# A hybrid decoder layer on one core: bounded expert gathers, an fp32 half of the input projection, and one-hot matrices written by GpSimd

## The chip, the cores and the metric

The kernel runs on one core of a Trainium2 chip. The metric is the device time of one execution in microseconds (us), median of several runs. The engines are TensorE (PE; its weight loads are listed as PEld), VectorE (DVE), ScalarE (ACT), GpSimd (POOL) and SyncE (SP), which here issues most of the DMAs.

## The reference, cut to what matters

256 tokens of width 2048 go through a token mixer and then through an expert mixer. Matrices are fp32.

```python
h = modulate(rms_norm(x, g_pre_mix), sh1, sc1)          # shifts, scales, gates: silu(c) @ w_mod + b_mod
proj = h @ w_in                                          # 2048 x 4096
lru_x, lru_g, conf_v, conf_g = split(proj)               # 1024 columns each
y_lru = rg_lru(conv4(lru_x)) * gelu(lru_g)               # scan over time
z = silu(layer_norm(conv31(conf_v * sigmoid(conf_g))))
x = x + gt1 * rms_norm(concat([y_lru, z]) @ w_out)
h = modulate(rms_norm(x, g_pre_ffn), sh2, sc2)
q = (h @ wq)                                             # 8 heads, 2 halves of 128
# per head: top 16 of each half's 128 keys, then top 16 of the 256 sums
expert = row * 128 + col                                 # 8 heads x 16 slots = 128 experts a token
act = einsum(h, u_table[expert]); w = softmax(gates) * gelu(act)
x = x + gt2 * rms_norm(sum(w * v_table[expert]))         # u, v tables: 16384 x 2048 each
```

## The kernel before

**Numbers.** TensorE runs plain fp32 matmuls at a low rate, so large products split each fp32 matrix: a rounded high part (`split`: ScalarE copies, line 94) and the rest as a low part (VectorE subtracts, line 95). A product is three matmuls per 128 rows of the contraction: high by high, high by low, low by high (lines 351, 352, 354 and 765, 766, 768).

**Modulation and projection (to about 355 us).** `modchunk` and `modfull` stream `w_mod` through fp32 matmuls (lines 251, 276). `hchunk` writes `xn`, the modulated input, and its halves `hH` and `hL`. Ten of the 32 column tiles of `w_in` are begun early (`begin`); the other 22 go through `proj`, which takes two slabs of eight contraction tiles each. `slab` loads 512 KB into a buffer of `fring` (four buffers, and a fifth lent from `yT`), splits it into buffers of `Hring` and `Lring`, and issues 24 matmuls. Between slabs, `modstep` advances the modulation. `conf` turns two tiles into a gated tile and runs 31 taps of a convolution on VectorE (line 422); `lru` does the recurrence; `confln` the layer norm. The outputs `zc` lie in the upper half of the same memory as `xn`, the running sum `zs` in its first tile. Then comes `w_out`.

**First half of the experts (about 484 to 1234 us).** Instead of gathering whole rows, the kernel multiplies all 16384 experts densely on the first 1536 columns of `u` (`upiece`: 128 expert rows in two pieces of six contraction tiles, into the table `S` of 128 x 128 scores a token), and gathers only the last 512 columns: per slot one indirect DMA from GpSimd (`gathers`, line 704, 128 rows of 2 KB) and one multiply-and-sum on VectorE (`dot`, line 710). A planner, executed while the program is written out, sets the order by hand for VectorE: every piece calls `fill` (304 calls), which counts calls in `clock[0]`, grants the gathers a credit in `clock[2]`, and then places steps of the top-k search (`topk`) and dots into the rest of the piece's time; a dot comes at least `LAG` = 3 calls after its gather. GpSimd runs its queue in order and starts a gather as soon as its index column `ei` is written and the last dot on its buffer is done. Buffers: six in `guS` and 30 lent from rows of `S` not yet written; `free` is a queue, first in first out; `retire` takes lent buffers back.

**Weight stage (about 1234 to 1415 us).** For four tokens at a time, `extract` loads the slots' column indices (`cold`) on all partitions, forms the column-by-slot one-hot matrix `cb`, on GpSimd for even chunks (line 917) and on ScalarE in two passes for odd ones (lines 914, 915), multiplies it by `S` (line 920, fp32) and lets VectorE pick the slot's row (line 924). `wbuild`, one group of 16 tokens later, needs the transpose, slots by columns: TensorE transposes `cb` (line 937), ScalarE copies it out (line 939), VectorE writes the weighted row one-hot `At` (line 944), TensorE multiplies (line 945, fp32), and ScalarE puts the token's weights into `S` (line 946). `mods` is the rest of the last modulation vector, 20 steps of a 512 KB load and four matmuls; from the ninth chunk on one step goes with every chunk.

**Second half (about 1415 us to the end).** `S`, now the weights, multiplies the dense part of `v` (line 1023); 512 columns are gathered (line 996) and added on VectorE (line 1005).

Outside the stretches that are ordered by hand, a scheduler orders each engine's instructions by priority when the program is built.

## Time and profile before

| | |
|---|---|
| median of 3 runs | 2002.36 us (2001.26 to 2014.05) |
| profiled execution, its own time | 1990.23 us |
| its span | 1988.5 us |
| TensorE busy, share of the span | 1827.9 us, 92% |
| VectorE | 1530.5 us, 77% |
| ScalarE | 972.3 us, 49% |
| GpSimd | 674.8 us, 34% |

The span runs from the first to the last instruction. Busy times are sums over stages with different limits, so the shares say little alone. Durations of matmuls include their pipeline; the distance from start to start is what one costs in a row. An fp32 matmul is listed as two records.

### The profile page before, as it was taken

Reading aid. Unit: us, or ns where it says so; the run is one execution under the profiler, and the core shown is the slowest. Engines: PE = TensorE matmul, PEld = TensorE weight load, DVE = VectorE, ACT = ScalarE, POOL = GpSimd, SP = SyncE. Lnnn points to the kernel's source line nnn. Section 1 sums busy time; section 2 is a strip of 40 time slices with the busy share of each in tenths; the row PEclk is TensorE's granted clock in tenths of the full one; section 3 lists DMA queues with packets and bytes.
Section 4 is the critical chain, followed back from the end, with each engine's and each line's share of the span. In section 5 each row is a group of like instructions: output and inputs, shape, how many; then the busy total and the mean of one; then the engine's idle time right before and its main releaser. Section 6 shows DMA issues by size and latency. Waiting matters only on the chain.

```text
span 1988.5 us, 34804 instructions
## 1 busy us (share of the span) xinstructions
PE 1827.9 (92%) x12408; PEld 1580.1 (79%) x12408; DVE 1530.5 (77%) x3834; ACT 972.3 (49%) x1512; POOL 674.8 (34%) x577
## 2 busy tenths in 40 slices
PE   7897999898949699999899999999999999999996
PEld 3675787685949699999899999789877777778874
DVE  3249999755729489999787775789788888888887
ACT  3244434743625355555455555567544444544453
POOL 0000000000061432323543442224377666666662
PEclk8999999998979799999999999999999999999998
DMA  9988868686776677778898887742499898888884
GB/s 326 373 313 320 281 229 317 262 287 245 230 239 195 216 252 256 261 244 280 289 300 274 290 289 221 212 139 81 131 319 329 327 324 310 313 300 316 311 303 161
DMA packets 174799, 530.07 MB, mean 267 GB/s; under 512 B 20753, under 2 KB 44449, under 8 KB 167201
## 3 DMA queue, kind: packets, MB, share of 16 engines
q1 hardware_dynamic: 132656, 391.50, 57.8%
q0 software_dynamic: 40960, 134.25, 20.0%
q8 instruction: 97, 1.59, 0.3%
q10 hardware_dynamic: 1008, 2.10, 0.3%
q14 instruction: 78, 0.63, 0.1%
HBM read 521.40 MB, written 6.37 MB: 265 GB/s over the span
## 4 chain that ended last, share of the span: by engine, by line
PE 55%; issue 16%; POOL 11%; DMA 9%; DVE 5%; ACT 2%; another core or an unknown queue 1%; POOLq 0%; SPq 0%; ACTq 0%; DVEq 0%
PE acc L765 11%; PE acc L766 11%; PE acc L768 11%; POOL S L996 7%; PE acc L354 4%; PE acc L351 4%; PE acc L352 3%; PE W L945 3%; PE modps L276 3%; PE G L920 2%; DMA PF<-in_w_mod_dram 2%; POOL sl L996 2%; DMA PF<-in_w_in_dram 2%; POOL sh L996 2%; DVE PF L422 2%
## 5 line engine op out<-in xcount | busy, mean ns | idle before, releaser
L765 PE MATMUL acc<-sh,sb 128*128 128x256 f32 x1792 | 453.4, 288 | 36.8 <-issue 23.2
L766 PE MATMUL acc<-sl,sb 128*128 128x256 f32 x1792 | 452.1, 287 | 0.3 <-issue 0.3
L765 PEld LDWEIGHTS acc<-sh,sb 128*128 128x128 f32 x1792 | 349.3, 195 | 42.0 <-issue 25.1
L766 PEld LDWEIGHTS acc<-sl,sb 128*128 128x128 f32 x1792 | 349.3, 195 | 2.3 <-issue 2.2
L94 ACT ACTIVATE sb<-R 128x768 fp32r<-128x768 f32 (+2 forms) x203 | 196.8, 970 | 262.3 <-PE acc L766 115.2
L95 DVE TENSOR_TENSOR sb<-S,sb 128x768 fp32r<-128x768 f32 (+3 forms) x272 | 219.8, 809 | 130.7 <-ACT sb L94 106.1
L768 PE MATMUL acc<-sh,sb 128*128 128x256 f32 x1792 | 269.3, 285 | 9.9 <-issue 9.3
L94 ACT ACTIVATE sb<-S 128x768 fp32r<-128x768 f32 (+3 forms) x274 | 207.4, 759 | 140.0 <-PE acc L766 85.9
L996 POOL DMA_INDIRECT S<-in_vg_dram,ei x158 | 212.7, 1346 | 112.3 <-DVE R L1005 82.5
L768 PEld LDWEIGHTS acc<-sh,sb 128*128 128x128 f32 x1792 | 240.0, 194 | 10.1 <-issue 9.1
L704 POOL DMA_INDIRECT R<-in_ug_dram,ei x111 | 112.5, 1013 | 390.7 <-DMA R<-in_ud_dram 252.3
L95 DVE TENSOR_TENSOR sb<-R,sb 128x768 fp32r<-128x768 f32 (+1 forms) x160 | 150.2, 939 | 109.7 <-ACT sb L94 64.7
L704 POOL DMA_INDIRECT S<-in_ug_dram,ei x145 | 147.0, 1014 | 246.8 <-DVE R L710 156.3
L1023 PE MATMUL o<-sl,sb 128*128 128x512 f32 x900 | 221.4, 394 | 9.9 <-DVE sl L95 8.2
L1023 PE MATMUL o<-sh,sb 128*128 128x512 f32 x888 | 219.0, 395 | 10.1 <-DVE sh L95 9.3
L1023 PEld LDWEIGHTS o<-sl,sb 128*128 128x128 f32 x900 | 166.6, 188 | 53.8 <-DVE sl L95 17.9
L1023 PEld LDWEIGHTS o<-sh,sb 128*128 128x128 f32 x888 | 165.8, 189 | 53.9 <-DVE sh L95 18.2
L94 ACT ACTIVATE PR<-PF 128x1024 fp32r<-128x1024 f32 (+2 forms) x99 | 85.0, 868 | 127.5 <-DMA PF<-in_w_in_dram 85.5
L1023 PE MATMUL o<-sb 128*128 128x512 f32 x516 | 126.8, 391 | 1.5 <-ACT sb L94 1.5
L1005 DVE SCALAR_TENSOR_TENSOR R<-S,R 128x512 f32<-128x512 f32 x157 | 117.3, 747 | 3.5 <-DMA S<-in_vg_dram,ei 0.7
L351 PE MATMUL acc<-sh,PR 128*128 128x256 f32 x412 | 107.4, 296 | 8.8 <-ACT PR L94 7.1
L1023 PEld LDWEIGHTS o<-sb 128*128 128x128 f32 x516 | 96.6, 188 | 23.2 <-ACT sb L94 2.8
(304 smaller groups left out, 3436.3 us busy)
## 6 DMA issues: line engine op xcount, KB each, us to landing
R<-in_vd_dram SPq DMA_DIRECT2D x128, 768.0 KB
PF<-in_w_mod_dram SPq DMA_DIRECT2D x86, 1024.0 KB
R<-in_ud_dram SPq DMA_DIRECT2D x132, 384.0 KB
S<-in_ud_dram SPq DMA_DIRECT2D x124, 384.0 KB
PF<-in_w_in_dram SPq DMA_DIRECT2D x44, 512.0 KB
PF<-in_w_out_dram SPq DMA_DIRECT2D x32, 512.0 KB
PF<-in_w_in_dram SPq DMA_DIRECT2D x40, 256.0 KB
sl<-in_w_mod_dram SPq DMA_DIRECT2D x20, 512.0 KB
```

What stands on the lines that cost most here:

```text
L94: nc.scalar.activation(h, src, AF.Copy)
L95: (eng or nc.vector).tensor_tensor(l, src, h, op=OP.subtract)
L276: nc.tensor.matmul(ps[32 * g:32 * g + 32, a // 4:(a + n) // 4], cs32[:, k, :], t[:, g * n // 4:(g + 1) * n // 4], start=k == k0, stop=k == ...
L351: nc.tensor.matmul(ps, h[:, k - k0, :], rh(k), start=first and k == k0, stop=False)
L354: nc.tensor.matmul(ps, l[:, k - k0, :], rh(k), start=False, stop=last and k == k1 - 1)
L704: nc.gpsimd.indirect_dma_start(out=g, out_offset=None, in_=A["ug"], in_offset=bass.IndirectOffsetOnAxis(ap=ei[:, tt, s_:s_ + 1], axis=0))
L765: nc.tensor.matmul(ps, uh[:, k - k0, :], hH(k), start=k == 0, stop=False)
L766: nc.tensor.matmul(ps, uh[:, k - k0, :], hL(k), start=False, stop=False)
L768: nc.tensor.matmul(ps, ul[:, k - k0, :], hH(k), start=False, stop=k == end - 1)
L996: nc.gpsimd.indirect_dma_start(out=g, out_offset=None, in_=A["vg"], in_offset=bass.IndirectOffsetOnAxis(ap=ei[:, tt, s_:s_ + 1], axis=0))
L1005: nc.vector.scalar_tensor_tensor(og[:, tt, :], g, wn[:, tt, s_:s_ + 1], og[:, tt, :], op0=OP.mult, op1=OP.add)
L1023: nc.tensor.matmul(out[tt][n], a[:, tt * 128:tt * 128 + 128], b[:, 512 * n:512 * n + 512], start=r == 0 and a is wh and b is vh, stop=r == ...
```

## The change

- `gathers` stops when `out_max()` gathers are without their dot in the planner's order: six up to call 60, then one more every six calls. A buffer that a dot has freed goes to the front of `free`, so that the next gather takes it.
- In `proj` the first slab of a column tile is multiplied in plain fp32, from the loaded buffer and from `xn`, without a split (`slab32`); the second as before. `xn` must therefore live through the projection: `zs` gets memory of its own, and the fifth buffer of `fring` falls away.
- `extract` forms every `cb` on ScalarE. In `wbuild` GpSimd writes the slots-by-columns matrix `Bt` directly, four compares of 128 x 128 a chunk, from the column index of each slot (a fourth block of `trs`); the transposes and ScalarE's copies are gone. Their PSUM goes to `pG` and `pW`, three buffers each. `rawR` has five buffers, not six.
- A step of `mods` goes with every second chunk, so the 20 steps end with chunk 46, counted from 0, of 64, not 27.
- The transposes into `trs` come in two groups, three blocks that need no dot, and then the dots.

```diff
...
+OUT0 = 6
+OUTC = 60
+OUTS = 6
...
     zc = yT[:, CT:, :]
     spare = [[v[:, a:a + 4, :].rearrange("p a b -> p (a b)").rearrange("p (k c) -> p k c", c=128) for a in at]
-             for v, at in ((yT, (4,)), (yH, (8, 12)), (yL, (8, 12)))]
+             for v, at in ((yH, (8, 12)), (yL, (8, 12)))]
     zrow = PF.t(512, dt=BF)[:1]
     nc.gpsimd.memset(zrow, 0.0)
     ar = Area(0, RKB)
...
     xpR = tr_(2, T + LK - 1)
     zR = tr_(3, T + CK - 1)
     mx = ar.t(T)
+    zs = ar.t(T)
     psA = ExitStack()
     pp = psA.enter_context(pool("pp", NPP, space=PSUM))
...
         for k in range(k0, k1):
             nc.tensor.matmul(ps, l[:, k - k0, :], rh(k), start=False, stop=last and k == k1 - 1)
+    def slab32(ps, src, k0, k1, rhs, first, last):
+        w = fring()[:, :k1 - k0, :]
+        with tc.high_priority(offset=HP):
+            nc.sync.dma_start(w, src[:, k0:k1, :])
+        for k in range(k0, k1):
+            nc.tensor.matmul(ps, w[:, k - k0, :], rhs(k), start=first and k == k0, stop=last and k == k1 - 1)
     mring = lambda: wring().rearrange("p a b -> p (a b)")
     mods = itertools.chain(*(modfull(m, lambda: pp.tile([128, 512], F32, name="modps"), misc, mring, modsR, D, nc.sync)
                              for m in (2, 4, 3)))
...
                         begin(j - 1, i)
                 n += 1
         hchunk(j)
-    rings = fring, Hring, Lring
+    rings = Hring, Lring
     for r, more in zip(rings, spare):
         r.aps = r.aps + more
     for i in range(NFIRST):
...
             return begun.pop(ct)[:, (1 - i if ct >= 2 * CT else i) * T:][:, :T]
         ps = accum()
         for a in range(2):
-            slab(ps, A["w_in"][ct], a * KH, a * KH + KH, hH, hL, a == 0, a == 1)
+            if a:
+                slab(ps, A["w_in"][ct], KH, KT, hH, hL, False, True)
+            else:
+                slab32(ps, A["w_in"][ct], 0, KH, lambda k: xn[:, k, :], True, False)
             modstep(next(mcount))
         return ps
-    zs = yT[:, 0, :]
     lwa = PCOLS["lru_conv_w"][0]
     def conf(c):
...
     tops, free, dots, gone, lent, late = [], list(guS), [], [], {}, []
     clock = [0, 0.0, 0.0]
+    def out_max():
+        return OUT0 + max(0, clock[0] - OUTC) // OUTS
     def gathers():
-        while free and units and clock[2] > 0:
+        while free and units and clock[2] > 0 and len(dots) < out_max():
             clock[2] -= GU * 512 / 360
             g = free.pop(0)
             tt, s_ = units.pop(0)
...
         nc.vector.scalar_tensor_tensor(gjR(), g, 1.0, h2n[:, tt, :GU], op0=OP.mult, op1=OP.mult,
                                        accum_out=actg[:, tt, s_:s_ + 1])
         if not any(g is x for x in gone):
-            free.append(g)
+            free.insert(0, g)
         return dve(GU)
     def retire(r):
...
             gathers()
             dot()
     ta = Area(10, 16)
-    trs = [ta.t(3, 128) for _ in range(2)]
-    ra = Area(16, 18)
-    ri, rf = ra.t(2 * NK, dt=I32), ra.t(2 * NK)
+    trs = [ta.t(4, 128) for _ in range(2)]
+    ra = Area(16, 19)
+    ri, rf, cf = ra.t(2 * NK, dt=I32), ra.t(2 * NK), ra.t(2 * NK)
     nc.vector.tensor_scalar(ri, e2, 7, None, op0=OP.logical_shift_right)
     nc.vector.tensor_copy(rf, ri)
+    nc.vector.tensor_scalar(ri, e2, NK - 1, None, op0=OP.bitwise_and)
+    nc.vector.tensor_copy(cf, ri)
     for tt in range(2):
-        ps = misc()
-        for i, src in enumerate((rf[:, tt * 128:tt * 128 + 128], gt[:, tt, :], actg[:, tt, :])):
-            nc.tensor.transpose(ps[:, 128 * i:128 * i + 128], src, ident)
-        nc.scalar.activation(trs[tt], ps[:, :384].rearrange("p (a b) -> p a b", a=3), AF.Copy)
+        sl = slice(tt * 128, tt * 128 + 128)
+        for a, b, srcs in ((0, 3, (rf[:, sl], cf[:, sl], gt[:, tt, :])), (3, 4, (actg[:, tt, :],))):
+            ps = misc()
+            for i, src in enumerate(srcs):
+                nc.tensor.transpose(ps[:, 128 * i:128 * i + 128], src, ident)
+            nc.scalar.activation(trs[tt][:, a:b, :], ps[:, :128 * (b - a)].rearrange("p (a b) -> p a b", b=128), AF.Copy)
     nc.scalar.activation(tab, gt[:, 1, NK - 1:], AF.Gelu_apprx_tanh)
     psB.close()
...
     psM = ExitStack()
     pm = psM.enter_context(pool("pm", space=PSUM))
     pp = psM.enter_context(pool("ppM", space=PSUM))
-    pG = psM.enter_context(pool("pG", 2, space=PSUM))
-    pT = psM.enter_context(pool("pT", 2, space=PSUM))
-    pW = psM.enter_context(pool("pW", 2, space=PSUM))
+    pG = psM.enter_context(pool("pG", 3, space=PSUM))
+    pW = psM.enter_context(pool("pW", 3, space=PSUM))
     va = Area(0, 10)
     wn = va.t(2, NK)
     og = va.t(2, GV)
...
     ba = Area(0, 6, slot("h1", 6))
     wts = [[ba.t(128) for _ in range(3)] for tt in range(2)]
     TG = 4
-    rawR = Ring(ta.ring(3, TG, NK, dt=BF).aps + ba.ring(3, TG, NK, dt=BF).aps)
+    rawR = Ring(ta.ring(2, TG, NK, dt=BF).aps + ba.ring(3, TG, NK, dt=BF).aps)
     cbR = Ring([v for x in ("l2", "h2") for v in Area(0, 4, slot(x, 4, F32R)).ring(2, TG, NK).aps] + Area(0, 12, slot("b", 12, F32R)).ring(6, TG, NK).aps)
-    held = {}
     la = [Area(0, 6, slot(x, 6)) for x in ("l0", "l1")]
     mr = Ring([x.t(1024) for x in la])
     xiR = Ring([x.t(4, 128) for x in la])
...
     def extract(tt, t0, t1):
         tr, (aT, ge, wT) = trs[tt], wts[tt]
         for c0 in range(t0, t1, TG):
-            if c0 >= 32 or tt:
+            if (128 * tt + c0) // TG >= 8 and c0 // TG % 2 == 0:
                 next(mods, None)
             if c0 + tt and (128 * tt + c0) % 28 == 0:
                 next(turns, None)
             raw, cb = rawR(), cbR()
-            held[tt, c0] = cb
             nc.sync.dma_start(raw, cold[tt, c0:c0 + TG, :].rearrange("t s -> (t s)")[None, :]
                               .to_broadcast([128, TG * NK]).rearrange("p (t s) -> p t s", t=TG))
-            if c0 // TG % len(CBE) in [i for i, e in enumerate(CBE) if e == "A"]:
-                nc.scalar.activation(cb, raw, AF.Abs, bias=npart)
-                nc.scalar.activation(cb, cb.bitcast(F32), AF.Relu, scale=-1.0, bias=1.0)
-            else:
-                nc.gpsimd.tensor_scalar(cb, raw, ipart, None, op0=OP.is_equal)
+            nc.scalar.activation(cb, raw, AF.Abs, bias=npart)
+            nc.scalar.activation(cb, cb.bitcast(F32), AF.Relu, scale=-1.0, bias=1.0)
             G = pG.tile([128, TG, 128], F32, name="G")
             for i in range(TG):
                 nc.tensor.matmul(G[:, i, :].rearrange("p (b r) -> p b r", r=RB), cb[:, i, :].bitcast(F32),
...
                 nc.vector.scalar_tensor_tensor(jk2, iot, tr[:, 0, tl:tl + 1], G[:, i, :], op0=OP.is_equal,
                                                op1=OP.mult, accum_out=aT[:, tl:tl + 1])
         sl = slice(t0, t1)
-        nc.vector.tensor_tensor(aT[:, sl], aT[:, sl], tr[:, 2, sl], op=OP.add)
+        nc.vector.tensor_tensor(aT[:, sl], aT[:, sl], tr[:, 3, sl], op=OP.add)
         nc.scalar.activation(ge[:, sl], aT[:, sl], AF.Gelu_apprx_tanh)
-        nc.vector.tensor_tensor(wT[:, sl], ge[:, sl], tr[:, 1, sl], op=OP.mult)
+        nc.vector.tensor_tensor(wT[:, sl], ge[:, sl], tr[:, 2, sl], op=OP.mult)
     def wbuild(tt, t0, t1):
         tr, (aT, ge, wT) = trs[tt], wts[tt]
         for b in range(t0, t1, TG):
-            cb = held.pop((tt, b))
-            Tp = pT.tile([128, TG, 128], F32R, name="T")
+            Bt = BtR()
             for i in range(TG):
-                nc.tensor.transpose(Tp[:, i, :], cb[:, i, :], identr)
-            Bt = BtR()
-            nc.scalar.activation(Bt, Tp.bitcast(F32), AF.Copy)
+                nc.gpsimd.tensor_scalar(Bt[:, i, :], iot, tr[:, 1, b + i:b + i + 1], None, op0=OP.is_equal)
             Wp = pW.tile([128, TG, 128], F32, name="W")
             for i in range(TG):
                 At = AtR()
-                eng = nc.gpsimd if i >= TG - PAT else nc.vector
-                eng.tensor_scalar(At, iot, tr[:, 0, b + i:b + i + 1], wT[:, b + i:b + i + 1], op0=OP.is_equal, op1=OP.mult)
+                nc.vector.tensor_scalar(At, iot, tr[:, 0, b + i:b + i + 1], wT[:, b + i:b + i + 1], op0=OP.is_equal, op1=OP.mult)
                 nc.tensor.matmul(Wp[:, i, :], Bt[:, i, :], At, start=True, stop=True)
             nc.scalar.activation(S[:, :, tt * 128 + b:tt * 128 + b + TG, :],
                                  Wp.rearrange("p t (b r) -> p b t r", r=RB), AF.Copy)
```

## Rows read from the trace of the kernel before

**Rows 1.** Busy time of the engines by stretch: the projection, the weight stage.
```profile
140.00:355.00 215.00, 193.46 (x1420) 153.79 (x1418) 200.93 (x412) 91.61 (x124) 1.23 (x11) 0.96 0.81 291
1234.00:1415.00 181.00, 173.69 (x1492) 152.54 (x1491) 154.24 (x808) 117.80 (x223) 55.60 (x37) 1.00 0.47 136
```

**Rows 2.** The same view, first-half experts' stage: five stretches with and without gather bursts.
```profile
552.00:600.00 48.00, 20.03 (x129) 18.58 (x128) 8.24 (x23) 8.77 (x17) 31.03 (x32) 0.71 0.71 225
600.00:634.00 34.00, 34.00 (x275) 34.00 (x275) 33.38 (x154) 19.28 (x43) 0.00 (x0) 0.96 0.61 179
634.00:680.00 46.00, 26.96 (x175) 24.78 (x175) 19.12 (x58) 10.90 (x22) 28.24 (x27) 0.74 0.75 238
...
952.00:984.00 32.00, 27.05 (x204) 26.31 (x204) 24.25 (x58) 14.05 (x22) 19.10 (x17) 0.91 0.85 284
...
1100.00:1234.00 134.00, 133.49 (x1113) 133.28 (x1112) 89.32 (x165) 69.04 (x93) 48.34 (x48) 1.00 0.82 267
```

**Rows 3.** Chain that ended last, pieces in order: start us, us, what.
```profile
565.41 32.90 issue
...
1297.02 5.46 DMA sl<-in_w_mod_dram
...
1490.92 8.18 DMA S<-in_vg_dram,ei
```

**Rows 4.** Timeline of GpSimd and VectorE in the first-half experts' stage.
```profile
552.66 1.63 POOL L704 DMA_INDIRECT R<-in_ug_dram,ei  x1 [252.28 <-DMA R<-in_ud_dram]
...
592.18 0.95 POOL L704 DMA_INDIRECT S<-in_ug_dram,ei  x1 [0.30 <-issue]
...
1180.33 0.68 DVE L710 SCALAR_TENSOR_TENSOR R<-R,h2n 128x512 bf16<-128x512 f32 x1
...
1181.29 0.94 POOL L704 DMA_INDIRECT R<-in_ug_dram,ei  x1 [1.22 <-DVE R L710]
```

**Rows 5.** Timeline of TensorE: starts of split matmuls, then of fp32 ones.
```profile
1180.06 0.28 PE L765 MATMUL acc<-sh,sb 128*128 128x256 f32 x1
...
1180.18 0.28 PE L766 MATMUL acc<-sl,sb 128*128 128x256 f32 x1
...
357.66 1.03 PE L301 MATMUL misc<-R 128*128 128x256 f32 x4
358.52 0.59 PE L444 MATMUL misc<-R 128*128 128x256 f32 x2
```

**Rows 6.** Groups by line and form in the projection, 140 to 355 us.
```profile
L422 DVE SCALAR_TENSOR_TENSOR PF<-R,PF 128x256 f32<-128x256 f32 x240 | 106.3, 473 | 0.1
...
L95 DVE TENSOR_TENSOR PR<-PF,PR 128x1024 fp32r<-128x1024 f32 x30 | 36.4, 1217 | 1.6 <-ACT PR L94 1.6
```

**Rows 7.** Line 944 (durations min/median/max, first and last start), then 10 us of it.
```profile
L944 DVE TENSOR_SCALAR R<-iot,R,sh x256: 328/344/3065, 1246.2 to 1414.7; 128x128 f32<-128x128 f32 x128
...
1340.00:1350.00 10.00, 5.89 (x16) 1.00 0.31 92
```

**Rows 8.** All engines in those 10 us of the weight stage.
```profile
1340.00:1350.00 10.00, 10.00 (x91) 9.60 (x90) 9.40 (x52) 7.38 (x15) 3.17 (x2) 1.00 0.31 92
```

**Rows 9.** Groups by line: two of the weight stage, one of GpSimd later.
```profile
L944 DVE TENSOR_SCALAR R<-iot,R,sh 128x128 f32<-128x128 f32 x256 | 94.1, 389 | 7.7 <-PE W L945 6.7
...
L937 PE MATMUL T<-identr,sb 128*128 128x128 f32 x144 | 22.4, 263 | 0.0
...
L95 POOL TENSOR_TENSOR sb<-S,sb 128x128 fp32r<-128x128 f32 x2 | 1.0, 518 | 12.7 <-ACT sb L94 12.7
```

**Rows 10.** Timeline of the weight stage: GpSimd's instructions and VectorE's beside them.
```profile
1360.42 1.56 POOL L917 TENSOR_SCALAR sl<-R,ipart 128x512 fp32r<-128x512 bf16 x1 [3.06 <-issue]
...
1361.95 3.43 POOL L95 TENSOR_TENSOR sl<-R,sl 128x1536 fp32r<-128x1536 f32 x1
...
1360.64 0.55 DVE L944 TENSOR_SCALAR R<-iot,R,sh 128x128 f32<-128x128 f32 x1
...
1362.40 3.06 DVE L944 TENSOR_SCALAR R<-iot,R,sh 128x128 f32<-128x128 f32 x1
```

More of the change, by code (lines that the diff above doesn't have):

```diff
@@ L48 @@
 GTS = ((16,) * 8, (16,) * 7 + (8, 4, 4))
-PAT = 0
 KB = ((0, 1), (1, 3), (3, 6), (6, 9), (9, 12), (12, 14), (14, 16))
@@ L59 @@
 KSPL = 6
-CBE = "PA"
 TLAG = 3
```

## The prediction, made before the change was run

> **What bounds the kernel now.** I read the table of busy time by stretch first, then the chain of waits and the timelines inside the stretches that the change touches. The shares over the whole span hide that three stages have three limits.
>
> In the projection, 140 to 355 us, VectorE is busy 200.9 of 215 us and TensorE 193.5 [rows 1]: VectorE sets the pace, TensorE is close behind.
>
> In the first half of the experts, a split matmul starts 0.12 us after the one before [rows 5]. So the number of matmuls in a stretch, times 0.12, is the time it needed. From 1100 to 1234 us, 1113 matmuls need 133.6 of 134 us; from 600 to 634 us 275 need 33 of 34. But 552 to 600 us has 129, worth 15.5 of 48 us; 634 to 680 us 175, worth 21 of 46; 952 to 984 us 204, worth 24.5 of 32 [rows 2]. Lost: 32.5 + 25 + 7.5 = 65 us. In these three stretches GpSimd is busy 31, 28 and 19 us with gathers, and in the one from 600 to 634 us it has none [rows 2]. The first burst is 32 gathers back to back, from 552.66 to 592.18 us [rows 4], right after the first 32 slots are known; in the middle of it the chain shows 32.9 us in which VectorE waits for nothing that the profile names [rows 3]. It goes on at 598.3, some five microseconds after the last gather. A burst of 256 KB each 1.25 us, beside the dense loads, starves whatever else comes by DMA, and all three holes sit on such a burst. The granted clock falls to a mean of 0.71 and 0.74 in the two long holes [rows 2], part at 2.4 and part at 1.2 GHz, after TensorE had stood still: that is inside the 65 us.
>
> In the weight stage, 1234 to 1415 us, TensorE is busy 173.7 of 181 us, VectorE 154.2, ScalarE 117.8, GpSimd 55.6 [rows 1]. In a quiet stretch of it TensorE is busy 10.0 and VectorE 9.4 of 10 us [rows 8], in which 16 tokens get their `At` [rows 7]: 0.625 us a token, with 0.59 of VectorE work. Both are at their limit.
>
> **Bounded gathers.** Following the planner's rules through its 304 calls, old and new, gives nearly the same order of gathers and dots (all 256 placed by the last call, no tail). What differs is the turn of a buffer, from the dot that frees it to the dot of the gather that takes it: 39 to 45 calls in the first third before, 6 calls in the last third; now 4 to 9 calls up to call 64, some 20 by call 160, and 4 in the last 96 calls (86 dots). GpSimd's lead over VectorE is what that turn allows, since a gather waits for the dot on its buffer. With 36 free buffers it could run 32 ahead; now only the first six can go back to back, and each later one follows a dot. The old kernel shows the tied pattern late: a gather [rows 4] starts 0.27 us after the dot's accumulator read ends, one per piece, and there TensorE is full [rows 2]. So the 65 us should go. I take **-60 us**; the bounds are -68 (a smaller hole near 715 us too) and -45 (the first six gathers still hurt).
>
> The cover that this needs: a gather must land within its turn. At the end that is 4 pieces of 18 x 0.12 = 2.16 us, 8.6 us; less 0.76 for the dot and its read, 0.27 of wait and 0.94 of issue [rows 4], 6.7 us are left to land. Behind a dot that waits, VectorE's next low parts are queued, and TensorE waits for those.
>
> **The fp32 half.** Four fp32 records take 0.86 us from 357.66 to 358.52 us [rows 5], so one matmul of 256 columns, two records, 0.43 us, where the three split ones take 0.36. TensorE gains 22 tiles x 8 x 0.07 = 12.3 us of work. VectorE loses 22 subtractions of 1.217 us, 26.8 us [rows 6]; ScalarE as many copies, and was not the limit. VectorE falls to 174 us (its 240 recorded taps, 106.3 us [rows 6], stay), TensorE rises to 205.8: the bound changes hands, and the stage can't fall below about 206 of 215 us. I take **-9 us**. Bounds: -20, since the recorded 193.5 holds stretches at the lower clock (mean 0.96 [rows 1]) that a steadier TensorE would not have, and +12 if its old idle time of 21.5 us all stays. The lost fifth buffer, and buffers held until the matmuls are done, cost nothing as long as loads run three slabs ahead, some 9 us at 3.2 us a slab (half of 8 x 0.43 + 8 x 0.36, the modulation not counted); without that cover the +12 holds. DMA is busy 0.81 of the stage already [rows 1], so the moved loads fit, not by much. `zs` in its own memory changes no wait.
>
> **The weight stage.** Off TensorE go 256 transposes: 144 of them are busy 22.4 us [rows 9], 0.16 us each with their pipeline, so at most 40 us. ScalarE keeps its number of passes over 128 x 512 (32 chunks get two more, 64 lose a copy). VectorE keeps everything, so it now leads alone: 0.59 to 0.625 us a token, 256 x 0.60 = 154 us, and 12 us of ramp (1234 to 1246.2 us, the first `At` [rows 7]) make 166.
>
> GpSimd trades 32 compares of 512 columns for 256 of 128. The trace has no compare of that size. One of 512 takes 1.56 us [rows 10], a quarter is 0.39; a two-input instruction on 128 columns took 0.518 [rows 9]. The compare has one input, so I take 0.45, 115 us in all, under VectorE's 154. It is not on the path itself, as `Bt` needs only the index, and its three buffers let GpSimd lead by up to three chunks.
>
> But the two engines get in each other's way. Line 944 has a median of 344 ns [rows 7] and a mean of 389 [rows 9]: 45 ns x 256 = 11.5 us of delay. The rows beside each other show where: an `At` starts at 1362.40 us, under a GpSimd instruction of 3.43 us that started at 1361.95, and takes 3.06 us, until that one ends; another, under a compare that started at 1360.42 us, takes 0.55 [rows 10]. So 55.6 us of GpSimd [rows 1] cost 11.5, 0.21 per us; 115 us cost 24, 12 more than now. That gives 178 of 181 us, **-3 us**; bounds -15 (no further delay) and +52 (full exclusion, below).
>
> The Trainium skill, page "SBUF — State Buffer", section "Who interferes with whom", calls this an exclusive lock: VectorE's `tensor_scalar` in a two-port mode and any GpSimd instruction shut each other out for the whole instruction. Its 3.06 us row agrees; the 0.55 us row, which ended inside the 1.56 us compare, does not.
>
> The spread of the modulation: a 512 KB load took 5.46 us on the chain [rows 3], and such steps fell into the stage's first half. Two chunks now cover one step (8 tokens, 5 us), so the wait goes under, and VectorE's pace above is that of the quiet stretch. On SP's queue `w_mod` loads stand less thickly before the `cold` loads. The regrouped transposes into `trs` are worth under 1 us either way.
>
> **Sum.** -60 - 9 - 3 = -72 us. The profiled execution goes from 1990.2 to 1918 us. The median of the runs shown is 12 us above the profiled one, so I take the difference off the median: 2002.4 - 72 = **1930 us**. About 1%, 20 us, is what a measurement of this kernel can tell from no change.
>
> **Rivals.**
> *GpSimd and VectorE exclude each other fully.* Then a token of the weight stage costs one compare plus one `At`: 0.39 + 0.344 to 0.52 + 0.344 us, 188 to 221 us for 256, with the ramp 200 to 233 instead of 178: +22 to +55, middle +35, and the kernel takes 1965 us. For: the 3.06 us row. Against: the 0.55 us row, and the time in which VectorE works on line 924 and needs nothing of GpSimd's. Chance 0.2.
>
> *The bound does not do what it says.* If the 32.9 us without a named cause [rows 3] is not the burst but something that happens there anyway (the top-k's code coming in, say), the holes stay: 1990 us. Against it: three holes, three bursts, and the end of each tied to the end of the gathers. Chance 0.1.
>
> *The gathers come late* (slower). With a turn of 4 calls, a landing time over 6.7 us stalls VectorE at each of 86 dots. The chain has one wait of 8.18 us for a gather of `v` [rows 3]; if that were the rule, 1.5 x 86 = 129 us come back: 2059 us. Against: that is one of the longest pieces of the whole chain; from 1100 us on DMA is busy 0.82 [rows 2], and spread gathers find it free more often than a burst does. It decides from 6.7 us on. Chance 0.06.
>
> *The compare is cheap* (0.3 us or less) and TensorE's relief counts in full: -15 in the weight stage, -20 in the projection, 1907 us. Chance 0.04.
>
> The forecast keeps 0.6. The range that leaves out 2 in 10 runs from 1900 us (the good ends of the gathers' and the projection's bounds, the cheap case) to 1972 (the first rival's middle, or the bad ends of two terms). Under 1982 us: 0.6 + 0.2 + 0.04, less a little for the far end of the first rival, 0.83; within 1%: 0.11, most of it the second rival; slower by over 1%: 0.06.
>
> **What would show it.** Right: no run of more than six gathers in the timeline; from 552 to 680 us some 0.12 us a matmul and a granted clock of 1.00; the dense stage shorter by about 60 us; in the projection VectorE near 174 us of busy time and TensorE over 95% of the stretch; in the weight stage VectorE over 90% busy, line 944's mean at 0.43 us or so. Wrong: holes with no burst near them, VectorE waiting for gathers at line 710, ScalarE waiting for `w_in` loads, TensorE waiting for `Bt` from GpSimd, or line 944 near 0.6 us.

## The result, and the profile after

The changed kernel takes **1947.93 us** (median of 4 runs, 1946.42 to 1951.99) where the kernel before takes 2003.6 (4 runs, 2001.26 to 2014.05): a ratio of 0.9715, 95% interval 0.9678 to 0.9753. That lies inside the forecast range, 18 us above the forecast. The profiled execution went from 1990.23 to 1946.97 us, span 1945.2, granted clock 0.974.

Where these 43 us lie is read from four marks of the timelines: the start of the first matmul and of the last group of six matmuls of the dense expert stage, the start of the last copy into `S`, the end.

| stretch, us | before | after | difference | predicted |
|---|---|---|---|---|
| start to the first dense matmul | 496.4 | 478.2 | -18.2 | -9 |
| dense expert stage | 736.7 | 706.2 | -30.5 | -60 |
| weight stage | 182.5 | 187.9 | +5.4 | -3 |
| rest | 572.8 | 572.9 | +0.1 | 0 |

(The expectations below count the dense stage to the start of its last matmul, 0.6 us later.) The time fell into the range although no term was right: half of the largest went missing, the second was twice as large, and the third had the wrong sign.

**Busy time by stretch, after**; the columns are those of [rows 1, 2].

```profile
140.00:345.00 205.00, 200.67 (x1242) 154.31 (x1242) 187.63 (x411) 80.77 (x125) 1.37 (x11) 0.99 0.81 286
...
520.00:560.00 40.00, 36.37 (x291) 36.16 (x291) 28.63 (x133) 20.67 (x44) 9.37 (x9) 0.96 0.70 208
560.00:600.00 40.00, 37.42 (x310) 37.02 (x309) 35.72 (x152) 20.75 (x48) 17.40 (x17) 1.00 0.82 264
600.00:640.00 40.00, 30.98 (x238) 30.69 (x239) 26.36 (x98) 19.19 (x43) 12.78 (x15) 0.83 0.71 226
640.00:680.00 40.00, 34.31 (x266) 33.91 (x265) 29.36 (x117) 16.14 (x28) 16.17 (x17) 0.91 0.80 250
...
720.00:800.00 80.00, 72.84 (x571) 71.94 (x572) 63.80 (x246) 40.50 (x87) 28.68 (x29) 0.92 0.77 245
...
900.00:1170.00 270.00, 270.00 (x2253) 270.00 (x2252) 210.79 (x468) 144.71 (x199) 118.69 (x116) 1.00 0.90 296
```

In the projection TensorE is now the limit, 98% busy. The dense stage from 900 us on is full at 0.12 us a matmul. Before that, a full stretch of 40 us would hold 333 matmuls: 600 to 640 lacks 95, 640 to 680 lacks 67, and 720 to 800 us lacks 96 of 667; at 0.12 us each these are 31 us. The holes are smaller than before [rows 2], and still there.

**GpSimd's timeline, after**, around the one at 600 us:

```profile
565.36 0.94 POOL L721 DMA_INDIRECT R<-in_ug_dram,ei  x1 [4.37 <-DVE R L727]
566.61 0.94 POOL L721 DMA_INDIRECT R<-in_ug_dram,ei  x1 [0.30 <-issue]
...
589.69 1.69 POOL L721 DMA_INDIRECT S<-in_ug_dram,ei  x1 [1.59 <-ACT ei L702]
592.92 0.94 POOL L721 DMA_INDIRECT S<-in_ug_dram,ei  x1 [0.30 <-issue]
...
601.92 0.95 POOL L721 DMA_INDIRECT S<-in_ug_dram,ei  x1 [0.30 <-issue]
...
606.92 0.94 POOL L721 DMA_INDIRECT R<-in_ug_dram,ei  x1 [0.30 <-issue]
```

From 558 to 587 us the gathers come in pairs behind dots, as planned. Then 14 stand back to back, against 32 before [rows 4]. And VectorE's dots at that place:

```profile
590.48 0.67 DVE L727 SCALAR_TENSOR_TENSOR R<-R,h2n 128x512 bf16<-128x512 f32 x1
...
597.93 0.69 DVE L727 SCALAR_TENSOR_TENSOR R<-R,h2n 128x512 bf16<-128x512 f32 x1 [0.27 <-issue]
```

These are the first and the last of six in 8 us; one stands before them at 589.01, two follow at 604.09 and 604.81. So nine dots in 16 us let nine gathers go, into the buffers of `guS` (`R` in the rows): between two top-k stages VectorE's order has dots and nothing else beside the splits. The other five of the 14, at 589.69, 592.92, 598.17, 600.67 and 601.92 us, go to buffers lent from `S`. The first dot on such a buffer starts at 664.4 us, so these five wait for no dot. The bound let them through: it counts places in the planner's order, and GpSimd reaches its places long before VectorE. Counting gathers and dots in the two timelines, 11 gathers are without their dot at 606.92 us. The bound allows so many from call 90 on, and VectorE is then at its 52nd split, one a call.

**Groups of instructions, weight stage, after** (1185 to 1372 us), which answer to [rows 9], and busy time in its two parts:

```profile
L951 POOL TENSOR_SCALAR sh<-iot,R 128x128 f32<-128x128 f32 x256 | 153.3, 614 | 54.3 <-ACT R L874 33.2 <-PE W L956 20.2
L955 DVE TENSOR_SCALAR R<-iot,R,sh 128x128 f32<-128x128 f32 x256 | 101.8, 405 | 12.5 <-PE W L956 11.8
...
L956 PEld LDWEIGHTS W<-R,sh 128*128 128x128 f32 x512 | 78.3, 201 | 30.2 <-POOL sh L951 14.9 <-issue 10.0 <-POOL sl L96 3.1
```

```profile
1205.00:1275.00 70.00, 69.98 (x519) 51.48 (x518) 55.32 (x296) 49.17 (x90) 58.49 (x96) 1.00 0.67 201
1275.00:1365.00 90.00, 78.97 (x557) 70.92 (x556) 83.42 (x424) 54.24 (x98) 86.82 (x141) 0.94 0.22 65
```

GpSimd's compare takes 0.61 us, not 0.45. In the first part TensorE is full (the modulation's matmuls are there), in the second GpSimd is, 86.8 of 90 us, and TensorE's weight loads wait for it.

### The profile page after: what moved, and what is told of

Same layout as the page of the kernel before. It is cut to its first block, busy times and chain, and to the rows that moved or that the text cites. A ratio compares the mean times of both kernels' runs of the same rounds, so it can differ in the third digit from the quotient of the medians.

```text
span 1945.2 us, 34281 instructions
## 1 busy us (share of the span) xinstructions
PE 1823.4 (94%) x11978; PEld 1562.2 (80%) x11978; DVE 1513.3 (78%) x3814; ACT 957.8 (49%) x1493; POOL 779.9 (40%) x801
## 3 DMA queue, kind: packets, MB, share of 16 engines
q8 instruction: 95, 1.56, 0.3%
## 4 chain that ended last, share of the span: by engine, by line
PE 56%; issue 14%; POOL 12%; DMA 10%; DVE 5%; ACT 2%; another core or an unknown queue 1%; SPq 0%; POOLq 0%; ACTq 0%; DVEq 0%
PE acc L785 11%; PE acc L783 11%; PE acc L782 11%; POOL S L1007 6%; PE modps L278 3%; PE acc L353 3%; DMA PF<-in_w_in_dram 3%; DMA R<-in_vd_dram 3%; PE acc L356 3%; PE acc L354 3%; POOL sh L951 3%; PE acc L364 2%; PE W L956 2%; PE G L935 2%; POOL sh L1007 2%
## 5 line engine op out<-in xcount | busy, mean ns | idle before, releaser
L721 POOL DMA_INDIRECT R<-in_ug_dram,ei x158 | 157.6, 997 | 477.1 <-ACT ei L702 255.7
L1007 POOL DMA_INDIRECT S<-in_vg_dram,ei x158 | 217.2, 1375 | 116.1 <-DVE R L1016 85.8
L951 POOL TENSOR_SCALAR sh<-iot,R 128x128 f32<-128x128 f32 x256 | 153.3, 614 | 54.3 <-ACT R L874 33.2
L721 POOL DMA_INDIRECT S<-in_ug_dram,ei x98 | 99.8, 1018 | 138.6 <-DVE R L727 111.1
L95 ACT ACTIVATE PR<-PF 128x1024 fp32r<-128x1024 f32 (+2 forms) x81 | 66.2, 826 | 94.0 <-DMA PF<-in_w_in_dram 58.9
```

The costliest lines, as they stand in the source:

```text
L95: nc.scalar.activation(h, src, AF.Copy)
L721: nc.gpsimd.indirect_dma_start(out=g, out_offset=None, in_=A["ug"], in_offset=bass.IndirectOffsetOnAxis(ap=ei[:, tt, s_:s_ + 1], axis=0))
L951: nc.gpsimd.tensor_scalar(Bt[:, i, :], iot, tr[:, 1, b + i:b + i + 1], None, op0=OP.is_equal)
L1007: nc.gpsimd.indirect_dma_start(out=g, out_offset=None, in_=A["vg"], in_offset=bass.IndirectOffsetOnAxis(ap=ei[:, tt, s_:s_ + 1], axis=0))
```

## The experiments

All stand beside the kernel before on the same chip. The chips turned out to be of two kinds, which is the main finding: on some the kernel before takes about 2000 us, on others about 1916. (No chip was used at two different times, so the chip and the time of its use are not told apart; "kind of chip" means no more than this.) The table has every run; stretches are those above, in us.

| kernel | before, us | this, us | ratio, 95% interval | first dense matmul | dense | weight | rest |
|---|---|---|---|---|---|---|---|
| free | 1914.6 | 1903.2 | 0.9947, 0.9927 to 0.9966 | 475.1 | 659.7 | 188.5 | 570.1 |
| split | 1914.6 | 1923.0 | 1.0041, 1.0021 to 1.0060 | 498.9 | 666.5 | 188.4 | 572.7 |
| trans | 1914.6 | 1896.0 | 0.9913, 0.9891 to 0.9936 | 475.5 | 664.2 | 181.5 | 569.4 |
| paced | 1914.6 | 1904.5 | 0.9951, 0.9931 to 0.9970 | 477.7 | 660.9 | 187.1 | 576.2 |
| same | 1996.1 | 1939.9 | 0.9713, 0.9663 to 0.9763 | 474.9 | 701.7 | 191.2 | 571.2 |
| old | 1996.1 | 1993.7 (one run) | | 497.7 | 739.3 | 183.0 | 571.9 |
| mix | 1996.1 | 1936.9 | 0.9709, 0.9660 to 0.9758 | 477.4 | 703.1 | 182.6 | 570.3 |
| free2 | 1916.1 | 1898.5 | 0.9919, 0.9891 to 0.9948 | 474.5 | 660.4 | 189.0 | 570.0 |
| paced2 | 1916.1 | 1899.5 | 0.9906, 0.9877 to 0.9934 | 476.2 | 661.6 | 187.7 | 575.7 |
| pacedmix | 1916.1 | 1893.9 | 0.9889, 0.9857 to 0.9920 | 476.5 | 661.8 | 181.4 | 572.4 |
| half | 1996.5 | 1939.2 (one run) | | 477.5 | 694.0 | 189.1 | 576.9 |
| pacedmix2 | 1918.7 | 1894.6 | 0.9899, 0.9869 to 0.9930 | 475.5 | 659.9 | 182.1 | 573.2 |

**free: no bound.**

```
-        while free and units and clock[2] > 0 and len(dots) < out_max():
+        while free and units and clock[2] > 0:
...
-            free.insert(0, g)
+            free.append(g)
```

> The changed kernel without the bound, and with freed buffers at the end of the list again. Theory: the bound alone made the experts' dense stage 30.6 us shorter (737.4 to 706.8), so without it 1948 + 31 = about 1979 us, with one run of some 30 gathers back to back and a hole of 25 us or more under it. Rival: the dense stage gained because the projection handed over earlier, and the bound did little: under 1958 us.

Theory and rival can't be told apart by the time here, for the chip is another one: 1903 us, where the kernel before takes 1914.6, and the dense stage is 659.7 us, against 706.2 with the bound on the first chip. GpSimd's timeline has the burst whole, 32 gathers back to back:

```profile
531.49 1.66 POOL L721 DMA_INDIRECT R<-in_ug_dram,ei  x1 [252.14 <-ACT ei L702]
...
577.26 0.95 POOL L721 DMA_INDIRECT S<-in_ug_dram,ei  x1 [0.30 <-issue]
```

and the busy time under it has no hole: 333 matmuls in 40 us, at a DMA share of 0.98 and 350 GB/s.

```profile
560.00:600.00 40.00, 40.00 (x333) 39.69 (x332) 37.63 (x141) 21.14 (x39) 30.53 (x28) 1.00 0.98 350
```

So a burst of gathers beside the dense loads doesn't by itself starve TensorE. The prediction's cause for the holes needed something more.

**split: the fp32 half undone.**

```
-            if a:
-                slab(ps, A["w_in"][ct], KH, KT, hH, hL, False, True)
-            else:
-                slab32(ps, A["w_in"][ct], 0, KH, lambda k: xn[:, k, :], True, False)
+            slab(ps, A["w_in"][ct], a * KH, a * KH + KH, hH, hL, a == 0, a == 1)
```

> The changed kernel with both halves of the input projection split again. Theory: the 18.2 us by which the dense stage starts earlier come from the fp32 half, so it starts near 496 us again and the kernel takes 1948 + 18 = 1966 us; VectorE is back at about 200 us of busy time in the projection. Rival: part of the 18 is the same kernel's spread between runs (12 us between the fastest and the slowest run of before), and only the 9 us of the predicted sum come back: 1957 us.

The dense stage starts at 498.9 us, 21 to 24 later than in free, trans and paced on the same chip, and the kernel is 18.5 us slower than paced, 19.8 slower than free: the theory, rather more than less. In the stretch up to the output projection TensorE is idle for 23 of 226 us, and the granted clock is 0.94, against 0.99 in the changed kernel above:

```profile
140.00:366.00 226.00, 202.81 (x1444) 157.70 (x1443) 208.50 (x426) 101.56 (x143) 1.23 (x11) 0.94 0.79 285
```

**trans: the transposes back** (with ScalarE's copies, PSUM shared two by two by two again, and GpSimd's 512-column compares for every second chunk).

```
...
+            for i in range(TG):
+                nc.tensor.transpose(Tp[:, i, :], cb[:, i, :], identr)
             Bt = BtR()
-            for i in range(TG):
-                nc.gpsimd.tensor_scalar(Bt[:, i, :], iot, tr[:, 1, b + i:b + i + 1], None, op0=OP.is_equal)
+            nc.scalar.activation(Bt, Tp.bitcast(F32), AF.Copy)
...
```

> The changed kernel with the transposes, the copies of ScalarE and the 512-column compares back in the weight stage; the modulation stays spread out. Theory: GpSimd's 256 compares of 0.60 us set the pace of the second half of the stage, so without them the stage, now 187.3 us, falls to 170 to 178: the kernel takes 1932 to 1939 us. Rival: TensorE is the limit, and 256 transposes of up to 0.16 us come back: 200 us or more, 1960 us.

The weight stage falls to 181.5 us, 7.0 less than in free and 5.6 less than in paced: the direction of the theory, 3.5 us above its range. TensorE is full in its first half, as the rival had it, but full at a shorter time (in the next 80 us it is busy 76.7):

```profile
1160.00:1240.00 80.00, 79.70 (x688) 68.45 (x689) 69.15 (x366) 51.85 (x98) 22.96 (x15) 1.00 0.54 157
```

The stage of the kernel before took 182.5 us with the modulation bunched. So the spreading of it is worth 1 us, within what two chips may differ by.

**paced: each gather tied to VectorE's place.**

```
+            nc.vector.tensor_copy(ei[:, tt, s_:s_ + 1], ei[:, tt, s_:s_ + 1])
             nc.gpsimd.indirect_dma_start(out=g, out_offset=None, in_=A["ug"],
```

> The changed kernel with each gather's column of ei copied onto itself by VectorE first, in the planned order, so that a gather can't run before VectorE has come to its place (256 copies of some 0.07 us, 18 us of VectorE, which has 59 us free of 270 in the full stretch). Theory: the holes left between 500 and 800 us are gathers back to back, up to 14 at a time; paced, they come no faster than one per piece, the 45 us lost there fall to 15 or less, and the kernel takes 1915 to 1925 us. Rival: the holes belong to the ends of the top-k stages and stay: 1945 to 1955 us.

There were no holes to fill on this chip: the dense stage is that of free. As a test of the holes it says nothing; it shows that the copies cost the dense stage nothing. The rest is some 6 us longer with them; why is open. Nor does the bound gain anything on this chip: split and trans, which have it without the copies, take 666.5 and 664.2 us in the dense stage, free without it 659.7.

**same and old: both kernels unaltered, on another chip.**

> The changed kernel once more, unaltered, beside the kernel before on the same chip. In the four experiments before this one the kernel before took 1914.6 us, not 2003.6, and the dense stage had no holes, with the bound (in the variants with it) or without it. Theory: the holes belong to the chip and the bound only shortens them where they are; on a chip without them the change is worth the projection's part less the weight stage's, and takes 0.985 to 0.993 of the kernel before; on a chip with them 0.968 to 0.975, as in the result. Rival: the bound is worth the same everywhere, 0.97 on either.

> The kernel before, for its trace on the same chip. Theory: where it takes about 1915 us, its dense stage, 737 us in the result's trace, is 655 to 670 us though the first 32 gathers stand back to back; where it takes about 2003, the holes stand under them. Rival: the dense stage is 700 us or more either way, and the time went elsewhere.

This chip has the holes, and the ratio of the result, 0.9713. The trace of old, busy time:

```profile
555.00:600.00 45.00, 16.30 (x107) 15.35 (x106) 5.74 (x11) 6.40 (x11) 31.45 (x32) 0.68 0.77 238
600.00:634.00 34.00, 33.76 (x263) 33.77 (x264) 32.62 (x140) 19.91 (x44) 0.00 (x0) 0.92 0.57 163
634.00:690.00 56.00, 36.43 (x254) 34.93 (x254) 27.51 (x99) 17.33 (x39) 28.52 (x28) 0.79 0.74 231
```

The pattern of [rows 2] again, on the same two bursts. Old against same puts the change at -22.8 us up to the dense stage, -37.6 in it, +8.2 in the weight stage, -0.7 behind. The other half of the theory, 0.985 to 0.993 on a chip without holes, was not run for this kernel itself; free and paced, which differ from it only in the gathers, took 0.9947 and 0.9951 on one such chip, just over that range, and 0.9919 and 0.9906 on another. There the whole change is worth less than 1%.

**mix: Bt by TensorE and GpSimd in turn.**

```
+            if b // TG % 2 == 0:
+                cb = held.pop((tt, b))
+                Tp = pT.tile([128, TG, 128], F32R, name="T")
+                for i in range(TG):
+                    nc.tensor.transpose(Tp[:, i, :], cb[:, i, :], identr)
+                nc.scalar.activation(Bt, Tp.bitcast(F32), AF.Copy)
+            else:
                 for i in range(TG):
                     nc.gpsimd.tensor_scalar(...)
```

> The changed kernel with every second chunk of Bt made by TensorE's transposes and a copy of ScalarE, the others by GpSimd's 128-column compares; a quarter of the chunks gets its other one-hot from GpSimd's 512-column compare. Theory: with all chunks on GpSimd it sets the pace of the stage's second half, with all on TensorE that one is full (79.7 of 80 us); with half on each VectorE is left, 0.59 us a token: 256 x 0.59 = 151 us and 14 of ramp, the stage takes 165 to 173 us, 15 to 22 less than the changed kernel's 188. Rival: the waits between the engines cost more than the loads, 180 us or more.

The weight stage is 182.6 us, 8.6 less than in same; the rival's figure. Busy time of its second part:

```profile
1275.00:1355.00 80.00, 75.86 (x618) 70.54 (x616) 76.30 (x395) 53.85 (x101) 52.34 (x75) 0.98 0.25 73
```

GpSimd is off the limit; VectorE and TensorE are each at 95%. The theory took VectorE alone, at 0.59 us a token; what the 10 us above its range consist of isn't shown. As a whole the kernel is 3 us under same, inside their spread.

**free2, paced2 and pacedmix** were meant for a chip with holes and came to one without.

> The kernel without the bound again (it was run on a chip without holes, 1903 us), for a chip where the kernel before takes about 2000 us. Theory there: the bound is worth the 31 us of the result and the holes come back under 30 gathers back to back: 1965 to 1980 us and a dense stage of 730 to 740. Rival: the holes of the dense stage have another cause, and the bound, too, is worth nothing there: within 8 us of the changed kernel, 1935 to 1950. If the chip is again one without holes: 1903.

> The kernel whose gathers are paced by VectorE again, for a chip with holes. Theory: holes need gathers back to back; in the trace of this kernel they start 2.2 us apart, so the dense stage is 665 to 675 us there too, and the kernel takes 1905 to 1915. Rival: what counts is how much the transfers move in all, and the holes stay: 1935 to 1945. If the chip is again one without holes: 1904.

> Both alterations that helped, together: gathers paced by VectorE, and every second chunk of Bt by TensorE's transposes. Theory: they lie in different stages and add: 5 to 8 us under the paced kernel of the same call. Rival: what the weight stage gains is lost again behind it, where the pace is set by the loads of the value rows: within 2 us of it.

The dense stage is 660.4, 661.6 and 661.8 us, so unbounded, paced or not makes no difference there. The mixed `Bt` takes 5.6 us off paced2, as the theory has it.

**half: both kinds of gathers in one kernel**, so that a single trace of a chip with holes is enough.

```
-        while free and units and clock[2] > 0 and len(dots) < out_max():
+        while free and units and clock[2] > 0 and (units[0][1] < TOPK or len(dots) < out_max()):
...
+            if s_ >= TOPK:
+                nc.vector.tensor_copy(ei[:, tt, s_:s_ + 1], ei[:, tt, s_:s_ + 1])
...
-            free.insert(0, g)
+            free.insert(len(free) if s_ < TOPK else 0, g)
```

> Both kinds of gathers in one kernel, so that one trace of a chip with holes tells them apart: the first 32 gathers (slots 0 to 15 of each token tile) without the bound, with buffers taken in turn, the 224 others with the bound and paced by VectorE. Theory, on a chip where the kernel before takes about 2000 us: one hole of 20 to 33 us under the first 32 gathers, none behind it (83 or more matmuls in every 10 us from 610 us to 800 us, where the changed kernel lost some 30 us); 1925 to 1940 us. Rival: holes come at the ends of the top-k stages whatever the gathers do: near 600, 660 and 715 us again, 1955 to 1970. On a chip where the kernel before takes about 1915: no hole at all, 1895 to 1905.

It came to a chip with holes (1996.5 us before). Busy time, and GpSimd's gathers: the first and last of the 32 free ones, and two of those that are paced:

```profile
530.00:570.00 40.00, 19.68 (x146) 19.25 (x144) 10.33 (x39) 8.20 (x15) 27.28 (x28) 0.80 0.81 250
570.00:600.00 30.00, 21.53 (x163) 21.02 (x164) 19.44 (x82) 14.41 (x36) 4.13 (x5) 0.81 0.56 161
600.00:640.00 40.00, 40.00 (x333) 39.68 (x332) 38.40 (x144) 21.44 (x39) 0.00 (x0) 1.00 0.63 186
640.00:680.00 40.00, 40.00 (x333) 39.69 (x332) 38.02 (x175) 23.02 (x48) 15.08 (x15) 1.00 0.80 263
...
720.00:800.00 80.00, 79.83 (x664) 79.43 (x663) 76.17 (x338) 47.32 (x101) 34.02 (x36) 1.00 0.90 293
```

```profile
534.50 1.65 POOL L723 DMA_INDIRECT R<-in_ug_dram,ei  x1 [254.27 <-ACT ei L702]
...
574.41 0.94 POOL L723 DMA_INDIRECT S<-in_ug_dram,ei  x1 [0.30 <-issue]
...
676.88 0.94 POOL L723 DMA_INDIRECT S<-in_ug_dram,ei  x1 [1.21 <-DVE R L655]
679.04 0.94 POOL L723 DMA_INDIRECT R<-in_ug_dram,ei  x1 [1.22 <-DVE R L657]
```

One hole under the 32 gathers, none behind it: of the 19 stretches of 10 us from 610 to 800 us, 15 have the 83 matmuls or more that were expected, the others 80 to 82. From 530 to 600 us 309 matmuls stand where 583 have room: (583 - 309) x 0.12 = 33 us. Take them off the 694.0 and the dense stage is 661 us, that of the chips without holes. Of the rival's holes near 600, 660 and 715 us there is none, though top-k stages end there as well, at 616, 667 and 712 us. So on such a chip the gathers' spacing makes the holes, as far as one run can show it.

What stands still in the hole is read from half's timeline of all engines:

```profile
541.96 0.61 PE L834 MATMUL misc<-S 128*128 128x128 f32 x4
...
552.84 0.38 ACT L839 ACTIVATE R<-misc 128x256 f32<-128x256 f32 x1 [3.64 <-remote]
...
553.28 1.22 PE L834 MATMUL misc<-S 128*128 128x128 f32 x4 [10.23 <-issue]
...
555.79 0.41 PE L785 MATMUL acc<-sl,sb 128*128 128x256 f32 x1
...
560.63 0.38 ACT L839 ACTIVATE R<-misc 128x256 f32<-128x256 f32 x1 [7.41 <-remote]
...
577.47 0.84 ACT L95 ACTIVATE sb<-R 128x768 fp32r<-128x768 f32 x1 [16.45 <-remote]
578.36 0.58 PE L784 MATMUL acc<-sh,sb 128*128 128x256 f32 x1 [17.36 <-ACT sb L95]
...
580.37 0.96 DVE L96 TENSOR_TENSOR sb<-R,sb 128x768 fp32r<-128x768 f32 x1 [30.18 <-issue]
...
624.07 0.71 PE L834 MATMUL misc<-S 128*128 128x128 f32 x4
...
624.82 0.39 ACT L839 ACTIVATE R<-misc 128x256 f32<-128x256 f32 x1 [0.80 <-PE misc L834]
```

Read the pairs. In quiet, at 624 us, TensorE's score matmuls end at 624.78 and ScalarE copies their result at 624.82. In the hole they end at 542.57 and are copied at 552.84, 10.3 us later; the next set ends at 554.50 and is copied at 560.63, 6.1 later. ScalarE's split at 577.47 writes the high part into one of two buffers that take turns, so it needs the last matmul that reads the high part of the piece two before it. That one ended at 556.20, 21 us earlier. Its data are not what it waits for: their load was issued at 531.01 us, and from 553 to 581 us no packet of a dense load moves at all. VectorE stands still for 30 us, until 5 us after the last gather. In the other direction nothing is late: ScalarE ends at 553.22 and TensorE goes on at 553.28, at 578.31 and 578.36.

The trace also keeps the moments at which TensorE's semaphore is raised, by which the others learn that it has ended something. From 541 to 581 us eight such ends and eight raises stand in the same order. The raises come 3.6, 6.4, 10.2, 6.1, 21.2, 22.8, 21.4 and 19.5 us after the ends, the last three of them within 0.2 us, near 580.4. The waits above end within 0.1 us of their raise; in quiet a raise comes 0.015 us after the end. So what comes late is the end of TensorE's work, as the others learn of it. It goes with the kind of chip: of the 629 ends in the dense stage, 76 to 96 are raised more than 0.3 us late in each of the six traces from chips with holes (before, the changed kernel, same, old, mix, half), and in the eight others none but one, by 0.4 us. The spaced gathers of half keep some late raises, but from 600 to 800 us none by more than 2.2 us, and TensorE stays full.

The dense loads then have no free buffer to go to, which the DMA queues show, half from 541 to 575 us and free from 538 to 577:

```profile
q0 software_dynamic: 2222, 7.28, 69.4%
q1 hardware_dynamic: 451, 1.22, 11.0%
```

```profile
q0 software_dynamic: 2137, 7.01, 49.7%
q1 hardware_dynamic: 2540, 6.68, 47.6%
```

The gathers (q0) move no less in the hole, 214 GB/s against 180. The dense loads (q1) are down to a fifth although the DMA engines have room (a share of 0.81, then 0.56): they are not starved, they aren't asked for. Between 541 and 581 us SyncE issues two, at 541.76 and 549.60, each within 0.03 us of the end of the low part on VectorE that frees its buffer.

**pacedmix2: the best version once more.**

> Gathers paced by VectorE and every second chunk of Bt by TensorE's transposes, once more, for a chip with holes (on one without, the same kernel took 1893.9 us of 1916.1). Theory: no two gathers stand back to back for long, so the dense stage has no hole there either: 662 to 672 us, and the kernel takes 1892 to 1905 us, 0.945 to 0.955 of the kernel before. Rival: spread gathers hurt on such a chip too, a little each: 690 us or more, 1925 us or more. If the chip is again one without holes: 1894, and 0.989.

Again a chip without holes, and the same time as before on one, 1894.6 us. So the kernel paced all through was not run on a chip with holes. From half it can be estimated: span 1937.4, less the 33 us of its one hole, 1904 us, and some 6 less with the mixed `Bt`.

## Why the prediction was partly right

**Bounded gathers, -60 predicted, -30.5 and -37.6 measured.** The step that failed: "now only the first six can go back to back, each later one follows a dot". Five of 14 follow none, because the bound had grown in the planner's order and they had fresh buffers; the other nine follow dots, but these come nine in 16 us where the order has no top-k beside them. The prediction's own sign of being right, "no run of more than six gathers in the timeline", failed. "All three holes sit on such a burst" holds, and half shows that where the gathers are spaced the holes go. By its estimate of 661 us, spaced gathers would have been worth some 75 of the 736.7 us, more than the 60. "Starves whatever else comes by DMA" is wrong: free carries the same burst at 350 GB/s and loses nothing. What the chain called 32.9 us without a cause [rows 3] is VectorE waiting for an end of TensorE's: that wait ends at 598.31 us, 0.08 us after TensorE's semaphore is raised at 598.23, for a matmul that ended at 572.47. Why this happens on some chips and not on others no run here settles; nor whether the signal is late or TensorE itself, since the ends of matmuls in a trace are modelled.

**The fp32 half, -9 predicted, -18.2 measured, -22.8 between old and same, +21 to +24 when undone.** The mechanism was right: TensorE takes the lead, at 98%, and VectorE's work up to the output projection falls from 211.6 us in old to 185.3 in the changed kernel, 26.3 of the 26.8 that the prediction took off it. The term was mis-sized by its boundary. I took the stage to end at 355 us and asked how much faster its matmuls could go. They end at nearly the same time in both kernels: the last one starts at 342.9 and 341.4 us. What goes is what came behind them: the output projection waited for VectorE's backlog until it could start, at 369.8 us in old and at 342.6 us in the changed kernel, as TensorE's first rows of it show, after and old:

```profile
342.57 0.39 PE L353 MATMUL acc<-PR 128*128 128x256 f32 x1
```

```profile
369.79 1.01 PE L351 MATMUL acc<-PR 128*128 128x256 f32 x3
```

Part of the 27 us comes back later, as modulation steps that had filled the gap move into the output projection: from its start to the dense stage they take 20.7 us of TensorE in old and 29.1 in the changed kernel. The granted clock, 0.99 instead of 0.96, is the reason that the prediction gave for its bound of -20 and didn't take.

**The weight stage, -3 predicted, +5.4 and +8.2 measured.** The failing term is the compare: "I take 0.45, 115 us in all, under VectorE's 154". It takes 0.61, above the upper bound of 0.518, which came from the cost of a two-input instruction; "the compare has one input" was no ground for less. 256 of them, with the `v` splits and gathers that share the engine, fill GpSimd in the second part, and TensorE waits for `Bt`, one of the prediction's signs of being wrong. VectorE isn't over 90% busy, as it should have been, but 84% (156.7 of 187 us). The delay of VectorE was sized well: line 955's mean is 405 ns where 430 was forecast, so the first rival, full exclusion, falls. The two engines' timelines show which GpSimd instruction shuts VectorE out:

```profile
1293.53 3.42 POOL L96 TENSOR_TENSOR sl<-R,sl 128x1536 fp32r<-128x1536 f32 x1
1296.94 3.57 POOL L951 TENSOR_SCALAR sh<-iot,R 128x128 f32<-128x128 f32 x6
```

```profile
1293.59 3.45 DVE L955 TENSOR_SCALAR R<-iot,R,sh 128x128 f32<-128x128 f32 x1
1297.23 0.39 DVE L955 TENSOR_SCALAR R<-iot,R,sh 128x128 f32<-128x128 f32 x1
```

Under the two-input split an `At` takes as long as the split, 3.45 us; under the compares that follow, back to back, 0.39. The exclusive lock of the Trainium skill ("SBUF — State Buffer", section "Who interferes with whom") agrees with the first pair. The second it doesn't fit: GpSimd is in a compare at any moment there, and the `At` waits for no whole one.

**The other rivals.** Late gathers: no dot of line 727 waits for one, so this one falls. Holes that stay whatever the bound does: partly so, since 14 back to back still make them, but half refutes its cause, the top-k. The **sum**: -72 on paper, -43 in the profiled execution, -56 between the medians: the execution profiled before was 12 us under its median, the one after only 1. So the forecast of 1930 us came within 18 us by luck, by errors that partly cancel and by the choice of the execution that was profiled; its terms were 29 us off.

## What to carry to other kernels

A bound kept in a planner's order is not a bound in time: where transfers must be spaced, let each depend on something that the busy engine does at its place; one small copy was enough. When an engine gets relief, look at what stands behind its stage (here 27 us in which the output projection waited) and not only at the rate inside it. And read an unnamed wait from both sides, when the producer ended and when the consumer began, and on a second chip, before a resource is blamed for it.

## What the runs showed of the hardware

- Chips differ by more than this change: the same kernel before takes 1914.6, 1916.1 and 1918.7 us on some, 1996.1, 1996.5 and 2003.6 on others. Between traces of the changed kernel's kind the difference lies in the dense stage (701.7 us in same, 659.7 in free; the weight stage and the rest differ by 3 and 1 us).
- Where it is long, the ends of TensorE's work reach ScalarE up to 21 us late and VectorE up to 23 while gathers stand back to back (half), instead of 0.04 us, and in time again within 6 us after the last one. Where it is short, no end of the dense stage is more than 0.4 us late.
- A GpSimd compare of 128 columns takes 0.61 us; one of 512 took 1.56 [rows 10], so four small ones cost 2.4, half as much again.
- VectorE's copy of one int32 a partition takes 0.147 us, twice what I had put for it (half, 600 to 800 us):

```profile
L722 DVE COPY ei<-ei 128x1 int32<-128x1 int32 x68 | 10.0, 147 | 0.0
```
